# Seven block products instead of eight in a quarter of the gate and up projections of a transformer block on one Trainium2 core

## The chip, the cores and the metric

The kernel runs on one core of one Trainium2 chip. The time is device time in microseconds of one execution of the whole program. The engines are named as in the profile: PE (TensorE; PEld is its weight load), DVE (VectorE), ACT (ScalarE), POOL (GpSimd) and SP (SyncE, which here only issues DMAs).

## The reference

One encoder block on 256 rows of width 2048, in float32: a norm, four parallel mixers and an output projection, a cross-attention, and a gated feed-forward layer with 5632 hidden columns, then a last norm. The change lies in the feed-forward layer:

```python
def swiglu(h, w_gate_up, w_down):
    gate, up = jnp.split(h @ w_gate_up, 2, axis=-1)
    return (jax.nn.silu(gate) * up) @ w_down
```

Here `h` is 256x2048, `w_gate_up` 2048x11264 (5632 gate columns, then 5632 up columns) and `w_down` 5632x2048.

## The kernel before

**Products.** A float32 product is made of three matmuls on numbers rounded to a shorter type: each operand is a high part and a low part, and high*high + high*low + low*high are added in PSUM. For activations the two parts lie side by side in one tile of 512 columns: 256 columns high, 256 low (rows of `h` as columns). For weights ACT makes the high part `wh` (line 104) and DVE the low part `wl` (line 105).

**Weights.** All weight matrices come as one stream of 128x128 blocks in the order of use. A slab is 16 blocks (128x2048, 1 MB), loaded by SP into one of three `raw` buffers (line 83). Half a slab, 128x1024, is split at a time into one of three pairs of `wh` and `wl`. `take` (line 109) hands out 512 columns and sees to it that two more halves are written into the program ahead of the one in use.

**Gate and up.** `gate_up` (line 782) walks over 11 column blocks j of 512 hidden columns. For j = 0 gate and up run together in four PSUM banks (two row halves of 128 rows, and gate and up). For j = 1 to 10 first the gate block runs over all 16 inner blocks k, then the up block, each in two banks of the pool `psG`; `part_rows` (line 360) makes the three matmuls of 128x128 by 128x512 for one k and one row half. So one j has 16 k x 2 row halves x 2 (gate, up) x 3 = 192 matmuls. ACT turns the gate banks into silu (line 794); DVE multiplies them with the up banks (line 799, the operation in line 200), transposes the result in blocks (line 396), and POOL's queue stores it to the DRAM tensor `hidden` with four DMAs per row half (line 399).

**Down.** `down` multiplies with `w_down`, four column blocks c of 512, 44 inner blocks k each. The hidden activations are read back by `fetch` (line 803): a POOL DMA of 128x256 into `tmp`, then a split into a tile of `f` by ACT (line 204) and DVE (line 196). The first 28 of the 44 are read back during gate and up, the last 16 during down. At the top of `down` eight transposes of the residual go into two banks of the pool `psM` (line 889).

**Order.** Work that is not matrix product is written as generators, which `Background` (line 126) advances between products: `poll` runs a step when its due time has come and less than 0.9 us of DVE work is owed by the code's own count (`pe` takes time off, `dve` adds it); `drain` runs a generator to its end. That gives an order in the code. The tile framework then lays the instructions out on each engine with a planner of its own, and `keep_place` (line 222) pins instructions behind their predecessor where the planner is not to move them ahead.

Of the kernel before, what the change touches and what calls it, by code (L numbers as in the profile page):

```python
# [38 lines left out]
ROWS = ((0, 512), (704, 768), (880, 944), (NBLK - 48 * FT, NBLK))  # L39

LATE = 12

LAG, OWED, SOON = 1.3, 0.9, 0.01

NSC = 3
V_NG = 0
# [16 lines left out]
class Stream:  # L63
# [13 lines left out]
    def _half(self):  # L77

        nc, n = self.nc, 8 * len(self.halves)
        if n % 16 == 0:  # L80
            self.raw = self.rawp.tile([P, 2048], F32, name="raw", tag="raw")
            for a, b in zip(CUTS[n], CUTS[n][1:]) if n in CUTS else [(0, 1024), (1024, 2048)] if self.after else [(0, 2048)]:
                (nc.scalar if (n, a) == (0, 0) else nc.sync).dma_start(self.raw[:, a:b], self.W[n // 16][:, a:b])
                if self.after:
                    self.after.pop(0)()
        o = (n % 16) * P
# [12 lines left out]
        wh, wl = (pool.tile([P, 1088], F32R, name=t, tag=t) for t in ("wh", "wl"))  # L99
        at = 48 if any(a <= n < b for a, b in ROWS) else 8  # L100
        wh, wl = wh[:, at:at + 1024], wl[:, at:at + 1024]
        edges = [0, 256, 512, 1024] if n == 0 else [0, 512, 1024] if n == 8 else [0, 1024]
        for a, b in zip(edges, edges[1:]):
            nc.scalar.copy(wh[:, a:b], r[:, a:b])  # L104
            nc.vector.tensor_tensor(out=wl[:, a:b], in0=r[:, a:b], in1=wh[:, a:b].bitcast(F32), op=ALU.subtract)  # L105
        self.bg.dve(1024)
        self.halves.append((wh, wl))

    def take(self, w, k, c, nb=1):
        if self.n % 8 == 0:  # L110
            ahead = self.n // 8 + 1 + min(3 if self.extra else 2, self.n // 16)
            while len(self.halves) < min(ahead, NBLK // 8):
                self._half()
# [54 lines left out]
class Block:  # L168
# [191 lines left out]
    def part_rows(self, p, r, slot, wh, wl, start, stop, narrow=False):  # L360

        if narrow:
            for c in (slice(0, R), slice(R, 512)):
                self.part_rows(p[:, c], r, slot, wh[:, c], wl[:, c], start and c.start == 0, stop)
            return
        hi, lo = slot[:, r * P:(r + 1) * P], slot[:, R + r * P:R + (r + 1) * P]
        self.nc.tensor.matmul(p, hi, wh, start=start, stop=False)  # L367
        self.nc.tensor.matmul(p, hi, wl, start=False, stop=False)  # L368
        self.nc.tensor.matmul(p, lo, wh, start=False, stop=stop)  # L369
        self.bg.pe(0.68 * wh.shape[1] / 512)  # L370
# [399 lines left out]
    def mlp(self):  # L770
        tc, nc, act = self.tc, self.nc, self.act
        with tc.tile_pool(name="fp", bufs=1) as fp:
            self.gap(fp, 192)
            f = act[4:12] + [fp.tile([P, 512], F32R, name=f"f{i}") for i in range(20)] + self.h3
# [7 lines left out]
    def gate_up(self, gp, f):  # L782

        nc = self.nc
        box, g, stored = {}, {}, []

        def norm():
            box["col"] = self.rstd_begin([[self.acc]], D)
            yield

        def gate(ps):
            for r in range(2):
                g[r] = gp.tile([P, 512], F32, name=f"g{r}", tag=f"g{r}")
                nc.scalar.activation(g[r], ps[r], AF.Silu, scale=box["col"][:, r:r + 1])

        def up(j, ps):
            for r in range(2):
                h, u = (gp.tile([P, 512], F32, name=n, tag=n) for n in ("h", "u"))
                self.stt(h, ps[r], box["col"][:, r:r + 1], g[r], ALU.mult, ALU.mult)
                self.store_turned(self.ff[j * 512:(j + 1) * 512, r * P:(r + 1) * P], u, h)  # L800
            stored.append(j)

        def fetch(k0, k1, ahead, pause):

            m = {}
            for k in range(k0, k1 + ahead):
                if k < k1:
                    while len(stored) <= k // 4:
                        yield
                    m[k] = self.tmp()  # L810
                    nc.gpsimd.dma_start(m[k], self.ff[k * P:(k + 1) * P, :])  # L811
                if k >= k0 + ahead:
                    mark = self.mark()
                    self.split(f[k - ahead], m.pop(k - ahead))
                    self.keep_place(mark)
                    self.have = k - ahead + 1
                    yield pause

        ready = [self.late, self.bg.add(norm())]
        turned = self.bg.add(self.turn())  # L820
        ps = self.gemm_rows("w_gate_up", [0, DFF], self.h3, parts=[range(12), range(12, 16)],
                            before=lambda n: n and [self.bg.drain(g) for g in ready])
        gate(ps[0])
        up(0, ps[1])
        early = self.bg.add(fetch(0, FT - 16, 3, 2.0))
        for j in range(1, DFF // 512):
            gate(self.gemm_rows("w_gate_up", [j * 512], self.h3)[0])
            up(j, self.gemm_rows("w_gate_up", [DFF + j * 512], self.h3)[0])
        for x in (turned, early):
            self.bg.drain(x)  # L830
        self.bg.add(fetch(FT - 16, FT, 6, SOON))

    def turn(self):

# [19 lines left out]
    def down(self, f):  # L854
# [650 lines left out]
```

## Time and profile before

| what | value |
|---|---|
| runs | 1485.33, 1485.05, 1487.88 us (median 1485.33) |
| profiled execution, span from first to last instruction | 1482.6 us |
| profiled execution, its own time | not given apart from the span; the fastest run shown is 2.45 us above it |
| gate and up, j = 1 to 10, and a few transposes | 798.9 to 1234.8 us |
| down | 1234.8 to 1474 us |
| PE busy over the span | 99% |
| DVE / ACT busy over the span | 64% / 52% |

Matmul rows give about 389 ns for each matmul, but matmuls are pipelined: the distance from one start to the next is what adds up. A line number in a group is often a helper's, so tiles and shapes tell the groups apart. Two idle figures are to be kept apart: idle time of DVE or ACT costs nothing as long as PE has work.

### The profile page before, as it was taken

To read this page: it belongs to the slowest core of one execution; us is meant where nothing else is said; L and a number is where in the kernel's file an instruction comes from. 1 tells how busy PE (TensorE), PEld (TensorE's weight loads), DVE (VectorE), ACT (ScalarE), POOL (GpSimd) and SP (SyncE) were. 2 spreads that over 40 slices of the span, in tenths; PEclk is the share of its full clock that TensorE was granted. 3 is DMA by queue.
4 is the path that set the end of the run, shared out by engine and by line. 5 is a ranking of instruction groups with operands and counts; after the bars stand their busy time and mean duration, and the time that the engine had idled before them with its cause. 6 is when DMAs were issued, how large, how long until landed. Compare 5 with 4: busy or idle time off the path is not lost.

```text
span 1482.6 us, 19388 instructions
## 1 busy us (share of the span) xinstructions
PE 1468.6 (99%) x7356; PEld 1242.4 (84%) x7356; DVE 944.4 (64%) x1378; ACT 764.0 (52%) x1136; POOL 161.6 (11%) x276
## 2 busy tenths in 40 slices
PE   9999999999999999999999999999999999999997
PEld 8778888898898888888888888888888888888886
DVE  6688668778777777877765554555554456444444
ACT  6565655467555656656544444444444445434344
POOL 0220100000000001200042401111110112000000
PEclk9999999999999999999999999999999999999999
DMA  9976554454546555544567766666666666555554
GB/s 359 343 258 213 199 195 162 162 177 166 185 138 215 191 180 201 198 171 154 187 197 245 243 213 216 222 225 227 207 206 215 225 223 224 187 192 195 199 196 145
DMA packets 56718, 306.08 MB, mean 206 GB/s; under 512 B 9486, under 2 KB 11183, under 8 KB 25009
## 3 DMA queue, kind: packets, MB, share of 16 engines
q1 hardware_dynamic: 45920, 281.11, 55.1%
q0 software_dynamic: 10272, 23.09, 5.3%
q8 instruction: 57, 0.93, 0.3%
q10 hardware_dynamic: 432, 0.66, 0.1%
q14 instruction: 37, 0.30, 0.1%
HBM read 291.18 MB, written 13.63 MB: 206 GB/s over the span
## 4 chain that ended last, share of the span: by engine, by line
PE 97%; DVE 1%; ACT 1%; DMA 0%; SPq 0%; issue 0%; DVEq 0%; ACTq 0%
PE pg L368 20%; PE pg L367 20%; PE pg L369 20%; PE pg L318 18%; PE pg L319 10%; PE pm L369 1%; PE pm L368 1%; PE pm L367 1%; PE pm L1006 1%; PE pg L315 1%; PE pg L316 1%; PE pm L763 1%; PE pm L736 0%; DVE wl L105 0%; DMA raw<-in_W 0%; PE pm L1386 0%
## 5 line engine op out<-in xcount | busy, mean ns | idle before, releaser
L105 DVE TENSOR_TENSOR wl<-raw,wh 128x1024 fp32r<-128x1024 f32 (+1 forms) x503 | 611.4, 1217 | 465.1 <-ACT wh L104 459.9
L104 ACT CAST wh<-raw 128x1024 fp32r<-128x1024 f32 (+1 forms) x503 | 523.8, 1043 | 584.5 <-PE pg L369 415.4
L368 PE MATMUL pg<-wl,act 128*128 128x512 f32 (+1 forms) x1170 | 455.6, 389 | 1.5 <-DVE wl L105 1.5
L367 PE MATMUL pg<-wh,act 128*128 128x512 f32 (+1 forms) x1170 | 456.5, 390 | 0.0
L369 PE MATMUL pg<-wh,act 128*128 128x512 f32 (+1 forms) x1170 | 455.4, 389 | 0.0
L318 PE MATMUL pg<-act,wh 128*128 128x512 f32 x1104 | 387.7, 393 | 2.9 <-DVE act L196 2.9
L319 PE MATMUL pg<-act,wl 128*128 128x256 f32 x1216 | 340.7, 280 | 0.0
L368 PEld LDWEIGHTS pg<-wl,act 128*128 128x128 f32 x1170 | 219.9, 188 | 48.2 <-DVE wl L105 3.1
L367 PEld LDWEIGHTS pg<-wh,act 128*128 128x128 f32 x1170 | 219.9, 188 | 47.1 <-issue 1.2
L369 PEld LDWEIGHTS pg<-wh,act 128*128 128x128 f32 x1170 | 219.8, 188 | 45.8
L318 PEld LDWEIGHTS pg<-act,wh 128*128 128x128 f32 x1104 | 207.3, 188 | 48.1 <-DVE act L196 3.3
L319 PEld LDWEIGHTS pg<-act,wl 128*128 128x128 f32 x1216 | 228.5, 188 | 0.8 <-DVE wl L105 0.5
L399 POOL DMA_DIRECT2D hidden<-u x88 | 56.9, 654 | 304.1 <-DVE u L396 302.4
L369 PE MATMUL pg<-wh,f 128*128 128x512 f32 x120 | 46.7, 389 | 0.0
L367 PE MATMUL pg<-wh,f 128*128 128x512 f32 x120 | 46.7, 389 | 0.0
L368 PE MATMUL pg<-wl,f 128*128 128x512 f32 x120 | 46.7, 389 | 0.0
L843 POOL DMA_DIRECT2D xrows<-tmp x48 | 27.7, 584 | 128.8 <-DVE tmp L840 124.2
L196 DVE TENSOR_TENSOR tmp<-pg,tmp 128x256 f32<-128x256 f32 x78 | 32.4, 417 | 4.5 <-ACT tmp L325 3.7
L315 PE MATMUL pg<-act,wh 128*128 128x256 f32 x112 | 31.6, 282 | 0.0
L316 PE MATMUL pg<-act,wh 128*128 128x256 f32 x112 | 31.4, 280 | 0.0
L811 POOL DMA_DIRECT2D tmp<-hidden x44 | 24.3, 559 | 60.8 <-DMA hidden<-u 44.9
L399 POOL DMA_DIRECT2D keys<-k x32 | 20.7, 655 | 81.4 <-DVE k L396 79.2
(293 smaller groups left out, 1201.1 us busy)
## 6 DMA issues: line engine op xcount, KB each, us to landing
raw<-in_W SPq DMA_DIRECT2D x246, 1024.0 KB, 5.0
raw<-in_W SPq DMA_DIRECT2D x11, 512.0 KB, 7.3
hidden<-u POOLq DMA_DIRECT2D x88, 64.0 KB, 3.2
tmp<-hidden POOLq DMA_DIRECT2D x44, 128.0 KB, 3.1
res<-in_xT SPq DMA_DIRECT2D x8, 512.0 KB, 7.6
k<-in_mem SPq DMA_DIRECT2D x8, 256.0 KB, 8.3
k<-in_x SPq DMA_DIRECT2D x8, 256.0 KB, 10.2
keys<-k POOLq DMA_DIRECT2D x32, 64.0 KB, 5.2
```

Of the source, the lines that this page charges most:

```text
L104: nc.scalar.copy(wh[:, a:b], r[:, a:b])
L105: nc.vector.tensor_tensor(out=wl[:, a:b], in0=r[:, a:b], in1=wh[:, a:b].bitcast(F32), op=ALU.subtract)
L196: self.nc.vector.tensor_tensor(out=out, in0=a, in1=b, op=op)
L315: self.nc.tensor.matmul(p[:, 0:R], wh, slot[:, 0:R], start=start, stop=False)
L316: self.nc.tensor.matmul(p[:, 0:R], wh, slot[:, R:512], start=False, stop=False)
L318: self.nc.tensor.matmul(p[:, :], wh, slot[:, :], start=start, stop=False)
L319: self.nc.tensor.matmul(p[:, 0:R], wl, slot[:, 0:R], start=False, stop=stop)
L367: self.nc.tensor.matmul(p, hi, wh, start=start, stop=False)
L368: self.nc.tensor.matmul(p, hi, wl, start=False, stop=False)
L369: self.nc.tensor.matmul(p, lo, wh, start=False, stop=stop)
L399: nc.gpsimd.dma_start(to[:, :, 32 * a:32 * a + 32], u[32 * a:32 * a + 32, :].rearrange("f (b t) -> f b t", t=32))
L843: nc.gpsimd.dma_start(to[:, :, c:c + 32], u[32 * a:32 * a + 32, :].rearrange("t (b f) -> t b f", f=32))
```

## The change

The inner dimension of gate and up is 16 blocks, that is 8 pairs of blocks. For j = 1 to 10 gate and up now run together, pair by pair, in four PSUM banks. Pairs 1 and 5 of the eight are no longer done as eight block products (2 row halves x 2 inner blocks x gate and up) but as the seven products of Strassen's scheme (in Winograd's form), each again three matmuls.

- The slabs of these pairs are not split in halves. `_forms` makes from the slab three of its own blocks and four sums of its blocks, each as high and low part, into single-buffered tiles `hb`, `lb`, `ht`, `lt`, with the sums in float32 in `t`.
- The sums of the activations that the scheme needs are made once, during j = 0, by `left`.
- Three of the seven products go straight into the banks of the result, four into four banks of their own, which `combine` adds up behind pair 5. So one j uses all eight banks; the two pools change roles from one j to the next.
- The end of each j (`finish`) adds the combined products to the result banks, then silu, product, transposes and stores; its steps are spread by `poll` over the start of the next j, and drained ahead of pair 1 of it.
- 16 of the 44 blocks of the hidden activations, not 28, are read back during gate and up, 28 during down; the tiles for 12 of them lie in the space that gate and up leave free.

```diff
+EARLY = 16
+GU = 16 * (40 + 16 + 16 + 32 + 16)
+SEVEN = (1, 5)
+def seven(slab):
+    j, i = divmod(slab - GU // 16, 8)
+    return 1 <= j < DFF // 512 and i in SEVEN
...
+    def _forms(self, raw):
+        nc = self.nc
+        hb, lb, ht, lt = (self.swp.tile([P, w], F32R, name=t, tag=t)
+                          for t, w in (("hb", 1536), ("lb", 1536), ("ht", 2048), ("lt", 2048)))
+        t = self.swp.tile([P, 2048], F32, name="t", tag="t")
+        blk = raw.rearrange("p (b c) -> p b c", b=4)
+        sub = lambda out, a, b: nc.vector.tensor_tensor(out=out, in0=a, in1=b, op=ALU.subtract)
+        nc.scalar.copy(hb, raw[:, 512:2048])
+        sub(t[:, 0:1024].rearrange("p (b c) -> p b c", b=2), blk[:, 1:4:2, :], blk[:, 0:1, :].to_broadcast([P, 2, 512]))
+        nc.scalar.copy(ht[:, 0:1024], t[:, 0:1024])
+        nc.vector.tensor_tensor(out=t[:, 1024:1536], in0=raw[:, 1536:2048], in1=t[:, 0:512], op=ALU.add)
+        sub(t[:, 1536:2048], raw[:, 1024:1536], t[:, 1024:1536])
+        nc.scalar.copy(ht[:, 1024:2048], t[:, 1024:2048])
+        sub(lb, raw[:, 512:2048], hb.bitcast(F32))
+        for a in (0, 1024):
+            sub(lt[:, a:a + 1024], t[:, a:a + 1024], ht[:, a:a + 1024].bitcast(F32))
+        self.bg.dve(5632, 6)
...
-            with tc.tile_pool(name="gp", bufs=2) as gp:
-                self.gate_up(gp, f)
+            with tc.tile_pool(name="sw", bufs=1) as sw, tc.tile_pool(name="gp", bufs=1) as gp:
+                self.st.swp = sw
+                self.gate_up(sw, gp, f)
...
+                f += [hp.tile([P, 512], F32R, name=f"g{i}") for i in range(FT - 16 - EARLY)] + self.h3
+                self.bg.add(self.fetch(f, EARLY, FT, 6, SOON))
...
+        def left():
+            for i in SEVEN:
+                t = [self.tmp() for _ in range(2)]
+                for x, k in zip(t, (2 * i, 2 * i + 1)):
+                    nc.scalar.activation(x, self.resk(k), AF.Copy, scale=self.gvec(V_NG + 32, k))
...
+        def unit(i, cs, ps, start, stop, c0, c1):
+            b11, b21, b22, u1, t3, t2, t4 = st.take_forms("w_gate_up", (2 * i, 2 * i + 1), c0, c1)
+            whole = lambda k, r: [self.h3[k][:, a + r * P:a + (r + 1) * P] for a in (0, R)]
+            formed = lambda n: [x[:, n * P:(n + 1) * P] for x in sums[i]]
+            for p, a, b, own in ((ps[0], whole(2 * i, 0), b11, True), (cs[0][0], whole(2 * i + 1, 0), b21, False),
+                                 (cs[0][1], formed(3), b22, False), (ps[1], formed(0), u1, True), (ps[2], formed(2), t3, True),
+                                 (ps[3], formed(1), t2, True), (cs[1][0], whole(2 * i + 1, 1), t4, False)):
+                self.part(p, *a, *b, own and start, own and stop)
+                self.bg.poll()
+        def combine(ps, s):
+            p1, p5, p7, p6 = ps
+            (g0, u0), (g1, u1) = s
+            m = gp.tile([P, 512], F32, name="m", tag="m")
+            nc.scalar.copy(g0, p1)
+            self.tt(m, p6, g0, ALU.add)
+            yield SOON
+            self.tt(u0, p5, m, ALU.add)
+            yield SOON
+            self.tt(g1, p7, m, ALU.add)
+            yield SOON
+            self.tt(u1, p5, g1, ALU.add)
+        def finish(j, cs, s, last):
...
+                if last:
+                    self.tt(s[r][0], cs[r][0], s[r][0], ALU.add)
+                nc.scalar.activation(s[r][0], s[r][0] if last else cs[r][0], AF.Silu, scale=box["col"][:, r:r + 1])
...
+        for j in range(DFF // 512):
+            cols = [j * 512, DFF + j * 512]
+            banks = [self.gbank, self.bank]
+            cs = [[banks[j % 2]() for _ in cols] for _ in range(2)]
...
+                if i == 1 and end:
+                    self.bg.drain(end)
+                if j and i in SEVEN:
+                    if i == SEVEN[0]:
+                        ps = [banks[1 - j % 2]() for _ in range(4)]
+                    unit(i, cs, ps, i == SEVEN[0], i == SEVEN[-1], *cols)
```

More of the change, by code (lines that the diff above doesn't have):

```diff
@@ L85, in _half @@
                     self.after.pop(0)()
+        if seven(n // 16):
+            self.halves += [self._forms(self.raw), None]
+            return
         o = (n % 16) * P
@@ L107, in _half, with take_forms, look @@
         self.halves.append((wh, wl))
+    def _forms(self, raw):
[15 more added lines that the diff above has]
+        self.bg.dve(5632, 6)
+        cut = lambda x, y: [(x[:, a:a + 512], y[:, a:a + 512]) for a in range(0, x.shape[1], 512)]
+        return cut(hb, lb) + cut(ht, lt)
+    def take_forms(self, w, ks, c0, c1):
+        assert self.n % 16 == 0 and seven(self.n // 16)
+        self.look()
+        forms = self.halves[self.n // 8]
+        for k, c in ((ks[0], c1), (ks[0], c0), (ks[1], c0), (ks[1], c1)):
+            self.order += [(w, k, c + i * P) for i in range(4)]
+        self.n += 16
+        self.halves[self.n // 8 - 2] = None
+        return forms
+    def look(self):
+        ahead = self.n // 8 + 1 + min(3 if self.extra else 2, self.n // 16)
+        while len(self.halves) < min(ahead, NBLK // 8):
+            self._half()
     def take(self, w, k, c, nb=1):
         if self.n % 8 == 0:
-            ahead = self.n // 8 + 1 + min(3 if self.extra else 2, self.n // 16)
-            while len(self.halves) < min(ahead, NBLK // 8):
-                self._half()
+            self.look()
         half, o = self.halves[self.n // 8], (self.n % 8) * P
@@ L365, in part_rows, with part @@
             return
-        hi, lo = slot[:, r * P:(r + 1) * P], slot[:, R + r * P:R + (r + 1) * P]
+        self.part(p, slot[:, r * P:(r + 1) * P], slot[:, R + r * P:R + (r + 1) * P], wh, wl, start, stop)
+    def part(self, p, hi, lo, wh, wl, start, stop):
         self.nc.tensor.matmul(p, hi, wh, start=start, stop=False)
@@ new lines, in combine @@
+        def combine(ps, s):
[12 more added lines that the diff above has]
+            if last:
+                yield from last
@@ L803, in fetch @@
[L803 to L817, printed above, removed]
+                g, h = s[r]
@@ new lines, in finish @@
+                if last:
+                    self.tt(h, cs[r][1], h, ALU.add)
+                    yield SOON
+            for r in range(2):
+                g, h = s[r]
+                u = gp.tile([P, 512], F32, name="u", tag="u", bufs=2)
+                self.stt(h, h if last else cs[r][1], box["col"][:, r:r + 1], g, ALU.mult, ALU.mult)
+                yield SOON
+                self.store_turned(self.ff[j * 512:(j + 1) * 512, r * P:(r + 1) * P], u, h)
+                yield SOON
+            self.stored.append(j)
@@ L819, in gate_up @@
         ready = [self.late, self.bg.add(norm())]
+        forms = self.bg.add(left())
         turned = self.bg.add(self.turn())
[L821 to L828, printed above, removed]
@@ L829, in gate_up @@
-        for x in (turned, early):
+        early = end = None
+        for j in range(DFF // 512):
+            cols = [j * 512, DFF + j * 512]
+            banks = [self.gbank, self.bank]
+            cs = [[banks[j % 2]() for _ in cols] for _ in range(2)]
+            last = None
+            if j == 1:
+                self.bg.drain(forms)
+                early = self.bg.add(self.fetch(f, 0, EARLY, 3, 2.0))
+            for i in range(8):
+                if j == 0 and i == 6:
+                    for g in ready:
+                        self.bg.drain(g)
+                if i == 1 and end:
[4 more added lines that the diff above has]
+                    unit(i, cs, ps, i == SEVEN[0], i == SEVEN[-1], *cols)
+                    if i == SEVEN[-1]:
+                        s = [[gp.tile([P, 512], F32, name=f"{n}{r}", tag=f"{n}{r}") for n in "gh"] for r in range(2)]
+                        last = combine(ps, s)
+                        self.bg.add(last)
+                    continue
+                for k in (2 * i, 2 * i + 1):
+                    for c in range(2):
+                        wh, wl = st.take("w_gate_up", k, cols[c], 4)
+                        for r in range(2):
+                            self.part_rows(cs[r][c], r, self.h3[k], wh, wl, k == 0, k == KT - 1)
+                            self.bg.poll()
+            if j == 0:
+                s = [[gp.tile([P, 512], F32, name=f"{n}{r}", tag=f"{n}{r}") for n in "gh"] for r in range(2)]
+            else:
+                self.bg.drain(last)
+            end = self.bg.add(finish(j, cs, s, last))
@@ L830, in gate_up @@
+        for x in (end, turned, early):
             self.bg.drain(x)
-        self.bg.add(fetch(FT - 16, FT, 6, SOON))
     def turn(self):
```

43 lines of the change are left out of this document (32 added, 11 removed).

## The prediction

> **What bounds the kernel now.** I read the page first, then the chain of work that ended last around the stage, then busy time by stretch, groups by shape, VectorE's timeline and the waits.
>
> ```profile
> span 1482.6 us, 19388 instructions
> PE 1468.6 (99%) x7356; PEld 1242.4 (84%) x7356; DVE 944.4 (64%) x1378; ACT 764.0 (52%) x1136; POOL 161.6 (11%) x276
> PEclk9999999999999999999999999999999999999999
> PE 97%; DVE 1%; ACT 1%; DMA 0%; SPq 0%; issue 0%; DVEq 0%; ACTq 0%
> ```
>
> ```profile
> 798.91 0.44 PE pm L889 x4
> 799.35 0.47 PE pg L367
> ...
> 1234.58 0.23 PE pg L369
> 1234.82 0.44 PE pm L889 x4
> 1235.26 0.24 PE pg L367
> ```
>
> The chain is PE for 97% of the span, at full clock throughout. j = 1 to 10 run on PE from 799.35 to 1234.82 with no wait: 435.47 us for 10 x 192 matmuls, 0.2268 us from start to start. One j takes 43.55 us, a pair of inner blocks 24 matmuls or 5.44 us, a half slab 2.72 us. A removed matmul is worth 0.2268 us as long as everybody else keeps up.
>
> The second thing in these rows matters as much. Line 889's eight transposes stand at the top of `down`; four of them ran at 798.91, 436 us ahead of their place in the code. So the planner lays work out by when it is ready, not by the order of the code.
>
> How busy the others are, in one j (columns: PE, PEld, DVE, ACT, POOL busy, clock, DMA share, GB/s), with and without reading back hidden activations, and in `down`:
>
> ```profile
> 1016.60:1060.20 43.60, 43.60 (x194) 36.12 (x193) 23.45 (x25) 19.25 (x22) 7.38 (x12) 1.00 0.64 217
> ...
> 1147.40:1191.00 43.60, 43.60 (x194) 36.12 (x193) 22.10 (x21) 18.02 (x18) 7.37 (x12) 1.00 0.64 217
> ```
>
> ```profile
> 1300.00:1360.00 60.00, 60.00 (x266) 49.70 (x265) 28.49 (x27) 24.27 (x26) 0.00 (x0) 1.00 0.57 193
> ```
>
> VectorE works 23.45 of 43.60 us (54%) and, as the timeline further down shows, idles 1.49 us ahead of each split. That spare half is what the change spends.
>
> **PE.** Per pair the change removes one product of eight, 3 matmuls; 2 pairs x 10 j x 3 = 60 matmuls x 0.2268 = **-13.6 us**. The new pair takes 21 x 0.2268 = 4.76 us, one j 42.19. Weight loads are one per matmul as before and 188 ns long (a row below), under the 227 of a matmul, so they do not take over.
>
> **VectorE per j.** Prices:
>
> ```profile
> L105 DVE TENSOR_TENSOR wl<-raw,wh 128x1024 fp32r<-128x1024 f32 x145 | 177.3, 1223 | 185.9 <-ACT wh L104 185.9
> L104 ACT CAST wh<-raw 128x1024 fp32r<-128x1024 f32 x144 | 150.8, 1047 | 213.2 <-PE pg L369 213.2
> L369 PEld LDWEIGHTS pg<-wh,act 128*128 128x128 f32 x577 | 108.3, 188 | 22.5
> L399 POOL DMA_DIRECT2D hidden<-u x72 | 46.5, 654 | 256.4 <-DVE u L396 254.7 <-issue 1.7
> L200 DVE SCALAR_TENSOR_TENSOR h<-pg,rc,g 128x512 f32<-128x512 f32 x18 | 12.6, 742 | 0.0
> L794 ACT ACTIVATE g<-pg,rc 128x512 f32<-128x512 f32 x18 | 12.3, 690 | 8.0 <-PE pg L369 8.0
> L396 DVE STREAM_TRANSPOSE u<-h 128x512 f32<-128x512 f32 x18 | 11.6, 683 | 0.0
> L196 DVE TENSOR_TENSOR f<-tmp,f 128x256 fp32r<-128x256 f32 x20 | 8.2, 417 | 0.0
> L204 ACT CAST f<-tmp 128x256 fp32r<-128x256 f32 x20 | 7.9, 402 | 0.0
> ```
>
> ```profile
> L196 DVE TENSOR_TENSOR res<-res,pg 128x512 f32<-128x512 f32 x2 | 1.3, 678 | 0.0
> ```
>
> From 417 ns at 256 columns and 1223 at 1024 a column costs 1.05 ns, so 1536 columns are an estimated 1.76 us; 512 columns are 0.68 (last row, one input in PSUM, as in `combine` and `finish`).
> - Removed: 4 half slabs, 4 x 1.22 = 4.9. Left: 12 x 1.22 = 14.7.
> - Added: forms of two slabs, each 3 x 1.22 + 2 x 0.68 + 1.76 = 6.8, together 13.6; four adds in `combine`, 2.7; four in `finish`, 2.7.
> - Unchanged: two products 1.48, two transposes 1.37, and up to four splits of read-back blocks, 1.67.
> - Sum 36.5, with splits 38.2, of 42.19 us: 87 to 91%; operations that follow at once overlap by about 0.08 (two products take 1.40, below, for 1.48), which makes it 81 to 85%. It fits, with 4 to 8 us left per j where 20 were.
>
> The step with a price that no row shows is the 1024-column subtraction that reads one block twice (a broadcast input). Bounds: 1.22, and 2.45 if it ran at half rate; I take 1.22, since its form differs from line 105 only in the addresses read. At 2.45 VectorE has 2.5 us more per j, which still fits.
>
> **ScalarE per j.** 12 x 1.05 + 2 x (1.47 + 2 x 1.05) + 2 x 0.69 for silu + 0.62 for one copy + 4 x 0.40 = 23.3 us of 42.19. The 1.47 (1536 columns) and 0.62 (512) go by 402 ns at 256 and 1047 at 1024. Beside PE: 0. If its cover were gone, 23.3 - 19.25 = 4 us per j.
>
> **When it must be done.** Time 0 is the last matmul of the j before.
>
> ```profile
> 1016.75 1.40 DVE L200 SCALAR_TENSOR_TENSOR h<-pg,rc,g 128x512 f32<-128x512 f32 x2
> 1018.07 1.29 DVE L396 STREAM_TRANSPOSE u<-h 128x512 f32<-128x512 f32 x2
> ...
> 1031.93 1.23 DVE L105 TENSOR_TENSOR wl<-raw,wh 128x1024 fp32r<-128x1024 f32 x1 [1.49 <-ACT wh L104]
> ```
>
> ```profile
> SPq L83 <- DVE wl L105: 821.4, 161, 12.3
> ```
>
> ```profile
> DMA to landing us min/median/max: 4.8/4.9/5.6
> ```
>
> SP waits only for a free slab buffer. The slab of pair 1 takes that of the slab three earlier (pair 6), whose second half is split two halves ahead of its use at -8.2, so by about -13.6 + 1.05 + 1.22 = -11.3; 4.9 us later, at -6.4, the new slab lies there. Pair 1 starts at 5.44. Within these 11.8 us VectorE owes: two half-slab splits 2.4, the three forms' sums and `lb` 4.4 (the first products need these), and the first add of `finish` 0.68, which frees the bank that pair 1 starts in. That is 7.5 of 11.8. By the end of pair 1 (10.2) it also owes the other two split steps of the forms 2.4, three adds 2.0, products and transposes 2.85 and the next half slab or two 2.4: 17.2 of 16.6 us, some 15.9 after overlaps. So the first deadline is loose and the second has 0.7 us to spare: this is the place where the change can fail. Pair 5 has only forms ahead of it, no `finish`.
>
> Here I choose. Lost per j at pair 1: at least 0, at most 4.6 (worked out in the first rival). The nearest row is the pair `h`, `h`, then `u`, `u` above: the code writes product, transpose, product, transpose, and the planner put the second product into the time in which the first transpose was not ready. With that and the four early transposes I take a planner that fills gaps, and 0.2 us per j for orders that fit badly: **+2.0 us**.
>
> **What moves.** Twelve of the read-backs go from gate and up to `down`: 12 POOL issues, 12 casts (0.40) and 12 splits (0.42) in a stage where VectorE has 28.5 of 60 us and POOL nothing to do: 0; uncovered, 12 x 0.42 = 5 us. Their tiles lie where gate and up's tiles were, the last of which are given back when the last stores have left: 8 x 0.654 = 5.2 us of POOL issues after the last transpose, so about 11 us into `down`, while block 16 is needed after 16 x 6 x 0.2268 = 21.8 us. On POOL's queue they stand behind those stores, as the last read-backs do now. `left` adds about 3.6 us of VectorE and 2.8 of ScalarE to j = 0: covered, 0. At the top of `down`, the second result bank is freed by `finish`'s third add, about 0.1 + 3 x 0.68 = 2.1 us after the last matmul; transposes (0.88 if all eight come here) and three matmuls (0.68) cover 1.6: **+0.5** (bounds 0, and 5.5 for the whole of `finish`). SP issues the same slabs; with no wait in its way, 0.
>
> **Sum.** -13.6 + 2.0 + 0.5 = -11.1: a span of 1471.5. The median of the runs is 2.7 us above the profiled span, so 1474.
>
> **Rivals.**
> (1) Slower: VectorE keeps the code's order at pair 1. There the whole of the forms stands ahead of `finish`, since the code owes 6.8 us from them and so polls none of `finish` until it is drained. Forms then begin after the split at -0.4 and some 2.7 us of leftover adds, at 2.3, end at 8.7 (6.4 with overlaps), and the first add at 9.4: pair 1 starts 4.0 late, and the half slab behind `finish` comes 0.6 late again. 4.6 x 10 - 13.6 = +32: 1518. Against it: the two reorderings above. It decides once more than 1.36 us per j is lost, and above 3 us waits the order must really be the code's. [...]
> (2) The order is filled, but VectorE, at 85%, slips by 0.5 to 1.8 us per j at the second deadline (a broadcast at half rate, or waits between dependent forms, would do it): about 1.0 x 10, so 1482.
> (3) The change brings less than its count: matmuls slow down as VectorE and ScalarE fill up. For: nothing; j with 23.45 and with 22.10 us of VectorE take the same 43.60. 5 ns per matmul over 1860 is 9 us: 1483.
>
> **Chances.** Forecast (1471 to 1478) 0.50; (2) 0.24; (1) and states between (1490 to 1518) 0.19; (3) 0.07. A difference under 0.2%, 3 us, can hardly be told from none: the three runs shown differ by that much. Faster: 0.50, 0.13 of (2) and 0.03 of (3); same: 0.07 and 0.03; the rest slower. The likeliest case's own range is 1471 to 1478. Downwards nothing is left beyond the 60 matmuls, 1471; upwards the range takes in (2), (3) and the lower part of (1), to 1500, and leaves out the rest of (1) and a little below.
>
> **What would show it.** Matmuls of the stage fewer by 60 and 42.2 to 42.4 us per j; VectorE 33 to 38 us busy in each; the wait of PE on `lb`, on `finish`'s adds and on `wl` behind pair 1 near zero. The chain leaving PE for VectorE ahead of pair 1, or `finish` standing behind the forms in VectorE's timeline, shows (1) or (2); a longer step between matmuls without waits shows (3). The read-backs should not appear in the chain in `down`.

## The result, and the profile after

| | median us | runs | lowest to highest |
|---|---|---|---|
| before | 1486.49 | 13 | 1485.05 to 1489.13 |
| changed | 1481.33 | 13 | 1477.87 to 1484.97 |

The ratio is 0.9966, with a 95% interval of 0.9956 to 0.9976: the change makes the kernel faster by 5.2 us. The forecast was 11.3 us (1485.33 to 1474). So the sign held, and so did the wide range, up to 1500; the forecast's own range, 1471 to 1478, did not, and more than half of the gain is missing. The sections below look for that half.

The page of the changed kernel: its span, the busy time of each engine, the granted clock in 40 slices, and the shares of the chain of work that ended last, by engine and by line.

```profile
span 1479.6 us, 19468 instructions
...
PE 1459.8 (99%) x7296; PEld 1230.8 (83%) x7296; DVE 1066.3 (72%) x1548; ACT 793.3 (54%) x1172; POOL 161.4 (11%) x276
...
PEclk9999999999999999999999999999999999999999
...
PE 75%; DVE 12%; DMA 8%; issue 3%; ACT 2%; SPq 0%; DVEq 0%; ACTq 0%
PE pg L370 18%; PE pg L422 11%; PE pg L423 11%; PE pg L421 11%; PE pg L371 10%; DMA raw<-in_W 8%; DVE wl L121 5%; PE pm L423 2%; PE pm L422 2%; PE pm L421 2%; DVE t L133 2%; DVE lt L133 2%; DVE lb L133 1%; PE pm L1145 1%; ACT wh L120 1%
```

The matmuls are fewer by 60 (7356 to 7296), as counted. But the chain, which was PE for 97% of the span, now leaves PE for VectorE (12%: the split of half slabs, `wl`, and the forms' `t`, `lt`, `lb`) and for the slab transfers (8%). (The lines have moved: the split of a half slab is now L120 on ACT and L121 on DVE, the three matmuls of a product are L421, L422 and L423, the forms' sums are L133.)

Where the stage ends, in the chain of the changed kernel (start us, us, what):

```profile
1231.06 0.24 PE pg L423
1231.30 0.87 PE pm L1028 x8
1232.17 0.23 PE pg L421
```

All eight transposes (line 889 before, 1028 now) stand at the top of `down`, and the next product follows at once. j = 1 to 10 start at 801.36 and end at 1231.30: 429.94 us for 1860 matmuls, which at 0.2268 us would take 421.85. **8.1 us are lost in these ten j.** The distances between successive starts of matmuls show the same: what they have beyond 0.2268 us, called PE's gaps from here on, adds up to 7.5 us, all of it at line 422, the first product of a half slab with its low part `wl`, and at the matmul right behind it.

So the balance of the two profiled spans, 1482.6 and 1479.6, is this. Gate and up with j = 0 and the eight transposes went from 480.4 us (754.9 to 1235.26) to 474.7 (757.5 to 1232.17): 5.7 us won. `down` took 247.3 before and 247.4 after. And the stage began 2.6 us later, which is lost before the first changed instruction; the last section comes back to that.

The list of waits over the changed kernel's run (engine, line, what was waited for: us in total, times, longest):

```profile
DVE t L133 <- DMA raw<-in_W: 58.7, 20, 5.2
ACT hb L134 <- DMA raw<-in_W: 55.3, 18, 7.3
...
PE pg L422 <- DVE wl L121: 4.3, 7, 1.5
...
PE pm L422 <- DVE wl L121: 2.7, 4, 1.1
```

The first two rows have no counterpart before. In every one of the 20 uses of the scheme VectorE stands at the forms' first subtraction and waits for the slab's transfer, 2.9 us on average; ScalarE does the same in 18 of them at the forms' first cast. The last two rows are PE's waits for `wl`.

Busy time in about one j and in a later one (columns as in the prediction):

```profile
931.00:975.00 44.00, 42.64 (x186) 34.42 (x185) 34.86 (x42) 21.84 (x27) 7.37 (x12) 1.00 0.63 215
1018.00:1060.00 42.00, 42.00 (x187) 34.79 (x186) 34.11 (x38) 21.77 (x23) 7.39 (x12) 1.00 0.66 234
```

VectorE is busy for 34 us of a j, within the 33 to 38 of the prediction; the second stretch has no gap on PE at all. The load is the one that was worked out. What is wrong is the order. One place shows it: the end of the first of these stretches. The changed kernel's timelines of ScalarE, VectorE and PE (start us, us, engine, line, operation; in brackets the idle time before it, and what ended it):

```profile
961.96 1.05 ACT L120 CAST wh<-raw 128x1024 fp32r<-128x1024 f32 x1 [3.21 <-DMA raw<-in_W]
...
963.22 0.58 ACT L899 COPY g<-pm 128x512 f32<-128x512 f32 x1
968.77 1.48 ACT L134 CAST hb<-raw 128x1536 fp32r<-128x1536 f32 x1 [4.98 <-DMA raw<-in_W]
970.15 1.05 ACT L136 CAST ht<-t 128x1024 fp32r<-128x1024 f32 x1
971.11 1.04 ACT L120 CAST wh<-raw 128x1024 fp32r<-128x1024 f32 x1
```

```profile
964.52 0.68 DVE L248 TENSOR_TENSOR m<-pm,g 128x512 f32<-128x512 f32 x1
968.79 1.23 DVE L133 TENSOR_TENSOR t<-raw 128x1024 f32<-128x1024 f32 x1 [3.59 <-DMA raw<-in_W]
...
972.93 1.22 DVE L121 TENSOR_TENSOR wl<-raw,wh 128x1024 fp32r<-128x1024 f32 x1
```

```profile
972.84 0.39 PE L421 MATMUL pg<-wh,act 128*128 128x512 f32 x1
974.20 0.50 PE L422 MATMUL pg<-wl,act 128*128 128x512 f32 x1 [0.97 <-DVE wl L121]
```

The slab of pair 7 landed just ahead of 961.96, when ScalarE cast its first half. Its second half lay there from then on, and by 964 ScalarE had nothing else to do. But the next instruction in its queue is `hb` of the following pair 1, whose slab lands only at 968.7. ScalarE stands 4.98 us, VectorE 3.59 us and, in the middle of `combine`, the other three adds with it. When the slab lands, `hb`, `ht`, three steps of `t` and three adds go first, the split of pair 7's second half ends at 974.15, and PE has waited since the product of 972.84.

The other gaps are alike. All ten places where PE waits for `wl` in these ten j lie at the third or the second half slab ahead of a pair with forms (the last half of pair 7 or the first of pair 0, the last of pair 3 or the first of pair 4). For six of them the trace gives the landing of the slab: it was there 9 to 13 us before PE came to it.

### The profile page after: what moved, and what is told of

Read it like the earlier page. It is cut to its first block, busy times and chain, and to the rows that moved or that the text cites. A ratio compares the mean times of both kernels' runs of the same rounds, so it can differ in the third digit from the quotient of the medians.

```text
span 1479.6 us, 19468 instructions
## 1 busy us (share of the span) xinstructions
PE 1459.8 (99%) x7296; PEld 1230.8 (83%) x7296; DVE 1066.3 (72%) x1548; ACT 793.3 (54%) x1172; POOL 161.4 (11%) x276
## 4 chain that ended last, share of the span: by engine, by line
PE 75%; DVE 12%; DMA 8%; issue 3%; ACT 2%; SPq 0%; DVEq 0%; ACTq 0%
PE pg L370 18%; PE pg L422 11%; PE pg L423 11%; PE pg L421 11%; PE pg L371 10%; DMA raw<-in_W 8%; DVE wl L121 5%; PE pm L423 2%; PE pm L422 2%; PE pm L421 2%; DVE t L133 2%; DVE lt L133 2%; DVE lb L133 1%; PE pm L1145 1%; ACT wh L120 1%
## 5 line engine op out<-in xcount | busy, mean ns | idle before, releaser
L121 DVE TENSOR_TENSOR wl<-raw,wh 128x1024 fp32r<-128x1024 f32 (+1 forms) x463 | 559.4, 1214 | 269.2 <-ACT wh L120 264.1
L120 ACT CAST wh<-raw 128x1024 fp32r<-128x1024 f32 (+1 forms) x463 | 480.6, 1042 | 473.7 <-PE pg L423 219.8
L422 PE MATMUL pg<-wl,act 128*128 128x512 f32 (+1 forms) x770 | 300.3, 390 | 4.4 <-DVE wl L121 4.3
L421 PE MATMUL pg<-wh,act 128*128 128x512 f32 (+1 forms) x770 | 300.8, 391 | 0.1
L423 PE MATMUL pg<-wh,act 128*128 128x512 f32 (+1 forms) x770 | 299.7, 389 | 0.0
L422 PEld LDWEIGHTS pg<-wl,act 128*128 128x128 f32 x770 | 144.6, 188 | 38.0 <-DVE wl L121 8.3
L421 PEld LDWEIGHTS pg<-wh,act 128*128 128x128 f32 x770 | 144.5, 188 | 31.9 <-issue 1.2
L423 PEld LDWEIGHTS pg<-wh,act 128*128 128x128 f32 x770 | 144.5, 188 | 29.9
L422 PE MATMUL pm<-wl,act 128*128 128x512 f32 x272 | 106.6, 392 | 2.8 <-DVE wl L121 2.7
L423 PE MATMUL pm<-wh,act 128*128 128x512 f32 x272 | 105.9, 389 | 0.0
L421 PE MATMUL pm<-wh,act 128*128 128x512 f32 x272 | 105.9, 389 | 0.0
L133 DVE TENSOR_TENSOR t<-raw 128x1024 f32<-128x1024 f32 x20 | 24.5, 1225 | 58.7 <-DMA raw<-in_W 58.7
L422 PEld LDWEIGHTS pm<-wl,act 128*128 128x128 f32 x272 | 51.1, 188 | 15.8 <-DVE wl L121 5.2
L134 ACT CAST hb<-raw 128x1536 fp32r<-128x1536 f32 x20 | 29.6, 1480 | 60.4 <-DMA raw<-in_W 55.3
L421 PEld LDWEIGHTS pm<-wh,act 128*128 128x128 f32 x272 | 51.1, 188 | 10.7
L423 PEld LDWEIGHTS pm<-wh,act 128*128 128x128 f32 x272 | 51.1, 188 | 10.3
L133 DVE TENSOR_TENSOR lt<-t,ht 128x1024 fp32r<-128x1024 f32 x40 | 48.0, 1216 | 0.0
```

The source lines that it names most:

```text
L133: sub = lambda out, a, b: nc.vector.tensor_tensor(out=out, in0=a, in1=b, op=ALU.subtract)
L134: nc.scalar.copy(hb, raw[:, 512:2048])
```

## The experiments

The theories, by the letters of the expectations. **W**: the planner put the forms' first cast and first subtraction too early in the two queues; both stand there until the slab has landed, and half slabs whose data is there stand behind them. **L**: VectorE has too much work in one j, above all in the first five, in which hidden activations are read back. **S**: the new structure itself (gate and up together, four or eight banks, the later read-backs) costs something. Ratios are to the kernel before, on the same chip, with their 95% interval.

### The forms pinned behind the half slab ahead of them

```diff
+        mark = len(nc.cur_bb.bb.instructions)
         nc.scalar.copy(hb, raw[:, 512:2048])
         sub(t[:, 0:1024].rearrange("p (b c) -> p b c", b=2), blk[:, 1:4:2, :], ...)
+        for x in nc.cur_bb.bb.instructions[mark:]:
+            if x.engine in self.behind:
+                self.tc.add_manual_dep(x, self.behind[x.engine], mybir.DependencyInfo(
+                    mybir.DependencyClass.NoSync, mybir.DependencyReason.DATA), reason="order")
...
         self.bg.dve(1024)
+        if n % 16 == 0:
+            self.behind = {x.engine: x.name for x in nc.cur_bb.bb.instructions[-2:]}
```

The two instructions may not be laid out ahead of the split of the first half slab of the pair before; no wait is added, only an order within a queue.

> The first cast and the first subtraction of a slab's forms are pinned behind the split of the first half slab of the pair before, so that they no longer stand early in their queues. Theory W (the queues of ScalarE and VectorE stand behind an operation that waits for its slab's transfer, 58.7 us in all, and the half-slab splits behind it come late): VectorE's waits for the slab fall under 10 us, PE's gaps in gate and up from 7.6 us to under 2, the time some 5 us below the changed kernel, a ratio of 0.992 to 0.9935 to the kernel before. Theory L (VectorE has too much work in one j, above all while hidden activations are read back): the waits go, the gaps stay, since the work is the same; 0.9966. Theory S (the new order by pairs, with four banks and all of the evacuation at the end of j, costs by itself): the gaps stay; 0.9966.

Measured: 1473.96 us, ratio **0.9912** (0.9898 to 0.9926), a span of 1471.9. Waits for the slab over the run:

```profile
ACT hb L137 <- DMA raw<-in_W: 5.4, 9, 2.1
...
DVE t L135 <- DMA raw<-in_W: 0.8, 1, 0.8
```

And VectorE's timeline at the same place of another j:

```profile
1008.51 1.23 DVE L121 TENSOR_TENSOR wl<-raw,wh 128x1024 fp32r<-128x1024 f32 x1 [1.49 <-ACT wh L120]
1009.66 1.22 DVE L135 TENSOR_TENSOR t<-raw 128x1024 f32<-128x1024 f32 x1
1010.80 1.75 DVE L135 TENSOR_TENSOR lb<-raw,hb 128x1536 fp32r<-128x1536 f32 x1
```

VectorE's waits for the slab fall from 58.7 to 0.8 us, ScalarE's from 55.3 to 5.4, PE's gaps in j = 1 to 10 from 7.5 to 0.3, and the time falls by 7.4 us against the changed kernel (1481.33 to 1473.96), a little more than W expected. VectorE is as busy as in the changed kernel. W stands: the same work in another order loses nothing.

### The new structure without the scheme

```diff
-SEVEN = (1, 5)
+SEVEN = ()
...
-            else:
+            elif last:
                 self.bg.drain(last)
+            else:
+                s = [[gp.tile([P, 512], F32, name=f"{n}{r}", tag=f"{n}{r}") for n in "gh"] for r in range(2)]
```

> No pair by seven products; all else of the change stays (order by pairs, four banks, the end of j in one piece, 16 blocks read back early). W and L: nothing waits and VectorE has no forms, so 0.999 to 1.001 of the kernel before, no gaps on PE. S: slower than the kernel before, up to 1.005, with gaps of some 7 us.

Measured: 1486.04 us, ratio 0.9996 (0.9987 to 1.0005), no gaps in the stage. S falls: gate and up together, the changing banks and twelve read-backs moved to `down` cost nothing that can be measured.

### The read-backs spread out

```diff
-                early = self.bg.add(self.fetch(f, 0, EARLY, 3, 2.0))
+                early = self.bg.add(self.fetch(f, 0, EARLY, 3, 12.0))
```

> The 16 early read-backs come with a pause of 12 us instead of 2, so their splits spread over most of the ten j. L: the gaps in the first four j go, at most 2 us are left in all; 0.9925 to 0.9935. W: the waits for the slab stay at 50 to 60 us, the gaps shrink a little where the queue behind the wait is shorter, to 4 to 6 us; 0.995 to 0.9965. S: 0.9966.

Measured: 1483.53 us, ratio 0.9979 (0.9971 to 0.9988). The waits over the run:

```profile
DVE t L133 <- DMA raw<-in_W: 70.3, 20, 5.5
...
ACT hb L134 <- DMA raw<-in_W: 65.1, 19, 7.2
```

PE's gaps grew from 7.5 to 12.0 us in the profiled execution (at 1486.59 us the longest of its eleven). L expected them at 2 us or less, W at 4 to 6: both were missed. Where the added gaps lie is shown two experiments further down.

### The scheme in pair 5 alone

```diff
-SEVEN = (1, 5)
+SEVEN = (5,)
```

> Only pair 5 of each j by seven products: 30 matmuls fewer, 6.8 us of PE, and 5.5 us less of VectorE's work per j than with two pairs. L: VectorE has 31 us of work in 42.9, no gaps: all 6.8 us arrive, 0.9954, as good as or better than two pairs. W: half of the waits (25 to 30 us) and about half of the gaps (3 to 4 us): 0.9975 to 0.998. S: the gaps stay at 7 us: 1.000.

Measured: 1480.09 us, ratio 0.9958 (0.9944 to 0.9971), gaps of about 0.9 us. The waits over the run:

```profile
ACT hb L134 <- DMA raw<-in_W: 15.6, 10, 2.8
DVE t L133 <- DMA raw<-in_W: 3.5, 4, 1.6
```

W's number here, which left part of the loss in place, was missed, and L's, 0.9954, was the one met: 30 matmuls are worth 6.8 us, and 6.1 (1486.15 to 1480.09) arrive. By itself this run can't tell less work from shorter waits; the first experiment, with the work of both pairs and no gaps, does. With one pair the planner happens to put the forms where they hardly wait, 3.5 us in ten uses against 58.7 in twenty. So the changed kernel, with two pairs, is as fast as one with the scheme in one pair: what the second pair saves on PE, 6.8 us, goes into its gaps.

### The early read-backs moved behind gate and up

```diff
-                early = self.bg.add(self.fetch(f, 0, EARLY, 3, 2.0))
+                pass
...
-        for x in (end, turned, early):
+        self.bg.drain(end)
+        early = self.bg.add(self.fetch(f, 0, EARLY, 3, SOON))
+        for x in (turned, early):
             self.bg.drain(x)
```

All read-backs are still done; none runs beside gate and up.

> Nothing is read back while j = 1 to 10 run: the 16 early blocks are read back all at once between gate and up and down, which makes that place longer by some 10 us and is not what is looked at. Looked at are PE's gaps from j = 1 to 10. If a wait for the slab is enough by itself (W alone): the waits stay at 50 to 60 us and the gaps at 5 to 7. If gaps need both the wait and a queue that is full (W with L): the waits stay at 45 to 60 us and the gaps fall to 2 or less.

Measured once: 1485.18 us, beside 1486.18 of the kernel before; part of it is lost at the crowded top of `down`, with two gaps of 1.39 us and matmuls 0.43 us apart behind them. What it was run for is the stage itself:

```profile
DVE t L133 <- DMA raw<-in_W: 58.0, 17, 5.4
...
ACT hb L134 <- DMA raw<-in_W: 53.1, 16, 6.9
```

The waits over the run are what they were, and PE's gaps in j = 1 to 10 are 6.3 us. L falls, also as a condition of W: the read-backs aren't needed for the loss.

But they add to it where the queues stand. In this run and in the one with the read-backs spread out, VectorE's operations in gate and up come in the same order, by the tiles that they read and write, and so do ScalarE's, once those of the read-back blocks are left out. Beyond 42.19 us for each j, j = 1 to 4 lose 6.4 us here and 6.2 there; j = 5 to 10 lose 0.2 us here, where nothing is read back, and 6.9 there, where nine blocks are. Whether it is the blocks' splits or their transfers isn't separated.

### VectorE and ScalarE in the order of the code

```diff
+        prev = {}
+        for x in nc.cur_bb.bb.instructions[first:]:
+            if x.engine in (mybir.EngineType.DVE, mybir.EngineType.Activation):
+                if x.engine in prev:
+                    self.tc.add_manual_dep(x, prev[x.engine], mybir.DependencyInfo(
+                        mybir.DependencyClass.NoSync, mybir.DependencyReason.DATA), reason="order")
+                prev[x.engine] = x.name
```

This pins every instruction of the two engines in gate and up behind the one that the code writes before it: the prediction's first rival, built.

> VectorE's and ScalarE's instructions of j = 1 to 10 are pinned in the order of the code. The prediction's first rival: pair 1 starts 4.0 us late and the half slab behind it 0.6 more in each j, 4.6 x 10 - 13.6 = +32 us, a ratio of 1.02. If waits of PE for the first adds of the end of j are shorter than that, 1.00 to 1.01. If the order does not matter, 0.9966.

Measured: 1496.54 us, ratio 1.0069 (1.0054 to 1.0084), the only version slower than before. VectorE's and PE's timelines at a new j's pair 1:

```profile
1075.54 2.35 DVE L133 TENSOR_TENSOR lt<-t,ht 128x1024 fp32r<-128x1024 f32 x2
1077.81 1.28 DVE L248 TENSOR_TENSOR g<-pg,g 128x512 f32<-128x512 f32 x2
...
1083.00 3.46 DVE L121 TENSOR_TENSOR wl<-raw,wh 128x1024 fp32r<-128x1024 f32 x3
```

```profile
1081.85 1.07 PE L421 MATMUL pm<-wh,act 128*128 128x512 f32 x4
...
1084.23 0.50 PE L422 MATMUL pm<-wl,act 128*128 128x512 f32 x1 [1.31 <-DVE wl L121]
```

Here `finish` (line 248) stands behind the forms, as the rival said, and the splits of the next half slabs behind `finish`. One j takes 43.90 us (862.27 to 1213.47 for eight), 1.71 above the 42.19 of its matmuls. But the rival had priced 4.6: 4.0 ahead of pair 1 and 0.6 behind it. Pair 1 starts in time, since PE began with its products that need no freed bank, and the loss lies at the half slab behind pair 1, as in the second row (1.31 us idle), some 1.4 us each. Another 6.0 us are one single gap at 818.7. It is the same loss with another transfer: in the code's order the cast of the first read-back stands ahead of the next `wh`, and ScalarE waits 14.1 us for its data.

```profile
823.54 0.40 ACT L256 CAST act<-tmp 128x256 fp32r<-128x256 f32 x1 [14.12 <-DMA tmp<-hidden]
```

### Only one engine pinned

```diff
-            if x.engine in self.behind:
+            if x.engine in self.behind and x.engine == mybir.EngineType.DVE:
```

This is the first experiment with VectorE's instruction alone pinned; the second of the pair has `Activation` in the place of `DVE`.

> As e1, but only VectorE's first subtraction of the forms is pinned, not ScalarE's cast. If VectorE's wait is what costs: gaps under 2 us, 0.991 to 0.993. If ScalarE's (the casts of half slabs stand behind it): VectorE's wait under 10 us, ScalarE's at 50 us and more, gaps 5 to 7 us, 0.996 to 0.997. If both: between.

> As e1, but only ScalarE's cast is pinned. If VectorE's wait is what costs: it stays at 50 to 60 us, gaps 5 to 7 us, 0.996 to 0.997. If ScalarE's: gaps under 2 us, 0.991 to 0.993. If both: between.

Measured: 1481.69 us with VectorE pinned, ratio 0.9969 (0.9958 to 0.998), gaps 7.3 us; 1482.39 with ScalarE pinned, ratio 0.9974 (0.9959 to 0.9989), gaps 10.7. Both are where the changed kernel is: each came out as the branch of its expectation in which the other engine's wait is what costs. The waits of the two, over the run:

```profile
ACT hb L137 <- DMA raw<-in_W: 60.3, 20, 5.9
...
DVE lb L135 <- ACT hb L137: 42.9, 20, 4.2
```

```profile
ACT ht L143 <- DVE t L135: 83.7, 18, 7.9
...
DVE t L135 <- DMA raw<-in_W: 62.9, 20, 7.8
```

Either engine alone held up the half slabs here. With VectorE free of the wait for the slab, ScalarE still stands at `hb`; `wl` needs `wh` from ScalarE, so the loss stays. With ScalarE pinned, VectorE stands at `t`, and ScalarE behind it at `ht`.

### A buffer of their own for the slabs of pairs 1 and 5

```diff
-            self.raw = self.rawp.tile([P, 2048], F32, name="raw", tag="raw")
+            pool, tag = (self.swp, "own") if seven(n // 16) else (self.rawp, "raw")
+            self.raw = pool.tile([P, 2048], F32, name=tag, tag=tag)
```

Nothing is pinned; the transfer of such a slab waits for the forms before it, about half a j earlier, and no longer for the split of a slab shortly before. To make room, 12 blocks instead of 16 are read back early.

> The slabs of pairs 1 and 5 are loaded into a buffer of their own instead of one of the three shared ones (and 12 blocks, not 16, are read back early, to make room). Nothing is pinned. If the waits come from a shared buffer that comes free too late: the slab lands earlier, VectorE's waits for it fall under 15 us, gaps under 2 us, 0.991 to 0.993. If they come from the planner placing the first subtraction where it believes the slab to be there, whenever that is: the waits stay at 30 us or more; the gaps may still shrink, because there is more time behind them.

Measured: 1473.79 us, ratio 0.9922 (0.9907 to 0.9937). The wait for the slab, over the run:

```profile
DVE t L134 <- DMA own<-in_W: 16.7, 10, 2.2
```

The wait is a little above the 15 us that were expected. No gap is left in j = 1 to 10 (one of 1.6 us stands in `down`). The loss is gone here with no pin, as W says it should be when the slab is earlier in memory. But the planner laid the queues out otherwise too (VectorE's order in gate and up is another one in most places), so the earlier slab isn't shown to be the cause by itself.

### Three pairs, pinned

The pin of the first experiment, with `SEVEN = (1, 3, 6)` and 14 early blocks.

> Pinned as e1, with three pairs (1, 3 and 6) by seven products (14 blocks read back early, to make room). PE: 30 matmuls fewer than e1, -6.8 us. VectorE per j: 36.5 + 6.8 - 2 x 1.22 = 40.9 us of work, some 38 after overlaps, of 40.8 us. If filling VectorE to that point costs by itself (L): gaps of 1 us and more per j, no faster than e1, 0.991 to 0.998. If only waits cost (W): 0.9865 to 0.988.

Measured: 1466.12 us (1464.18 to 1468.12), ratio **0.9869** (0.9852 to 0.9885), the fastest version. Busy time over eight j:

```profile
870.00:1206.00 336.00, 336.00 (x1484) 278.25 (x1483) 310.71 (x336) 186.36 (x190) 50.81 (x81) 1.00 0.64 223
```

VectorE is busy 310.7 of 336 us, 92%, and PE is never without work. The waits over the run are not gone:

```profile
ACT hb L137 <- DMA raw<-in_W: 31.9, 11, 3.8
...
DVE t L135 <- DMA raw<-in_W: 8.1, 10, 1.9
```

So here neither VectorE's load, 92%, nor a wait as such, 31.9 us in all on ScalarE, cost PE time. In the changed kernel a wait cost where a half slab that was due soon stood behind it, 7.5 us in the ten j.

## Why the prediction was right and wrong

**Right: PE's count.** 60 matmuls went, at 0.2268 us from start to start, and the rate stayed. With the gaps gone the first experiment wins 12.2 of the 13.6 us (1486.15 to 1473.96), and three pairs win 19.3 of 20.4. The third rival, matmuls that slow down beside fuller engines, is out: at 92% of VectorE the 336 us above hold 1484 matmuls, 0.2264 us each.

**Right: VectorE's prices and load.** The broadcast subtraction, for which 1.22 us was chosen between 1.22 and 2.45, takes 1.225 in the changed kernel's groups by shape (count, then total us and mean ns, then idle time before it and what ended it):

```profile
L133 DVE TENSOR_TENSOR t<-raw 128x1024 f32<-128x1024 f32 x20 | 24.5, 1225 | 58.7 <-DMA raw<-in_W 58.7
...
L134 ACT CAST hb<-raw 128x1536 fp32r<-128x1536 f32 x20 | 29.6, 1480 | 60.4 <-DMA raw<-in_W 55.3
```

The right-hand column, idle time on line 133, is the part that the price list left out.

**Right: what was costed at nothing.** The moved read-backs cost nothing (second experiment, 0.9996). That experiment leaves `left` out; in the changed kernel j = 0, where `left` runs, takes 44.2 us (757.15 to 801.36), as before (754.51 to 798.75). SP's slabs, put at nothing too, come back below. The top of `down` cost 0.1 rather than the 0.5 forecast.

**Wrong: "0.2 us per j for orders that fit badly: +2.0 us".** This term of the sum measured 7.5 us by the gaps and 8.1 by the length of the ten j. It was placed at pair 1's deadlines, the form sums and `finish` against a slab that lies there at -6.4 on the clock of the j before. In the place shown above the slab landed even earlier, at 968.7 against a last matmul at 976.6, so at -7.9; and pair 1 itself was not late. What failed is the assumption behind the term: that VectorE and ScalarE come to the forms when the slab is there, and until then do what is ready. They came to them 3.6 and 5.0 us before. The early transposes and the pair `h`, `h`, `u`, `u` were read as a planner that fills gaps and so as a reason for a small price. But at the row `[4.98 <-DMA raw<-in_W]` ScalarE filled nothing: it stood 4.98 us ahead of `hb`, while the slab of the `wh` cast behind it had landed before 961.96. VectorE stood 3.59 us with three adds behind its subtraction. In the code's order ScalarE stood 14.12 us at the cast of the first read-back. So what was laid out behind a late transfer came late in these places, in the planner's order as in the code's. That the planner goes by when it expects data to be ready, and lays the forms out for a slab that then comes later, is the author's estimate: what time it supposes for a transfer no view shows.

**A second part of it, the transfer.** The prediction took 4.9 us from issue to landing, the median before. In the changed kernel, between 842 and 1215 us:

```profile
DMA to landing us min/median/max: 4.8/6.3/8.9
```

and with the forms pinned, over the same stretch:

```profile
DMA to landing us min/median/max: 4.9/5.6/7.3
```

The SP queue of the changed kernel, at the place shown above, has the two slabs ahead of pair 1's:

```profile
955.53 0.33 SPq L96 DMA_DIRECT2D raw<-in_W  x1
...
956.62 0.33 SPq L96 DMA_DIRECT2D raw<-in_W  x1
```

Before, SP issued 8 slabs in 38.41 us, one each 5.5 us by the rate at which PE used them up. Now a buffer comes free after the forms' last subtraction and the next after a split, and the two transfers, issued 1.09 us apart, run beside each other; the one that pair 7 waited for was there, by the start of its cast, 6.4 us after its issue. So slabs land later, which lengthens the wait. How much of the 7.5 us this is was not taken apart.

**The rivals.** (1), the code's order, is right in kind: built, it is slower than before. Its price, 4.6 us per j, was 2.7 times the 1.71 measured (the single gap of 6.0 us, which it didn't foresee, stands apart), because it let pair 1 wait for banks that its first products don't need; the place that binds is the half slab behind pair 1, which the prediction named as the second deadline. (2) forecast 1482 us and the time is 1481.3, but not for its reasons: the broadcast is not at half rate, and VectorE at 92% keeps up where the order is right. The agreement is by chance.

**The base.** The sum was set on three runs, 1485.33; the median of 13 is 1486.49. In each run of the comparisons the time stands 1.8 us above its own span; the profiled execution before, with 1482.6, was thus a quick one of about 1484.4. The forecast's 2.7 us between span and median held 0.9 us for that, and the median of 13 asks for 1.2 more. So 1474 + 5.7 (8.1 rather than 2.0 in j = 1 to 10, 0.1 rather than 0.5 at the top of `down`) + 1.2 = 1480.9, beside 1481.3 measured.

**Open.** Why j = 1 to 4 lose time even with nothing read back, while later j with the same waits lose none; whether a read-back adds its gap by its splits or by its transfer; how much of the loss is the longer transfers; and what duration the planner assumes for a slab.

## What to carry to other kernels

When a planner lays out the queues, price a new operation that reads a transfer by what will stand behind it if the transfer is late, not by its duration and the engine's load: here a VectorE at 92% cost nothing, and two early instructions in each use cost 7.5 us, the gain of a whole pair (6.8). Look in the waits for operations that idle on a DMA in every use, and follow the queue behind them to work whose data has long been there. Then either pin the first instruction behind work that is due sooner, on every engine that has one (one of the two alone gained nothing here), or start the transfer earlier.

## What the runs showed of the hardware

**Behind some waits of PE, of 1.39 to 6.0 us, matmuls went on at about half their rate, and not in every execution.** Between 475 and 480 us, long before the change, PE waits 2.94 us in the kernel before and 2.95 in the changed one. What follows, by stretch, before and then after:

```profile
478.00:490.00 12.00, 11.53 (x66) 10.16 (x67) 9.27 (x20) 6.74 (x14) 0.00 (x0) 1.00 0.59 195
```

```profile
479.00:490.00 11.00, 10.46 (x51) 9.14 (x52) 6.73 (x15) 4.74 (x10) 0.00 (x0) 0.84 0.41 144
```

In the execution before the clock stays at 1.00; in the one after it is 0.84 over 11 us, and for some of them matmuls start every 0.43 us rather than every 0.23. That is 1.6 of the 2.6 us by which the stage began later (the other 1.07 went on the first slabs of the kernel). The profiles of five experiments show this drop too: 0.91 over 475 to 495 us with the forms pinned, without the scheme and with one pair, 0.83 with the read-backs spread out, and 0.84 over 479 to 490 with three pairs. The structure without the scheme, which has the drop, takes the time of the kernel before, which has none in its profile (0.9996). With ScalarE pinned and with the buffer of its own j = 1 starts at 798.90 and 799.20 us, in the other eight at 800.23 to 801.55; by that these two are estimated to be without the drop, and it belongs to the execution rather than to the change. With ScalarE pinned the clock falls at another place, after a gap of 2.71 us at 817.3:

```profile
817.00:821.00 4.00, 1.46 (x6) 0.86 (x6) 3.91 (x5) 2.69 (x3) 2.22 (x4) 1.00 0.29 79
821.00:825.00 4.00, 4.00 (x12) 3.12 (x11) 4.00 (x4) 2.58 (x3) 0.00 (x0) 0.57 0.85 314
```

A clock of 0.57 over 4 us is an estimated 3.4 us at half clock, and matmuls stand 0.43 us apart from 821.85 to 824.83. Behind the one 6.0 us gap of the code's order they stand 0.43 us apart from 826.80 to 831.06, and 0.23 from there on. The same follows two gaps of 1.39 us close together; in the run without read-backs beside gate and up they end at 1232.15 and 1234.57:

```profile
1234.00:1237.50 3.50, 2.93 (x7) 2.35 (x8) 3.50 (x12) 1.17 (x4) 3.45 (x6) 0.51 0.38 82
```

The clock of 0.51 goes with matmuls 0.43 us apart from 1235.59 to 1237.30. What decides whether the clock falls behind a wait is not shown: 2.94 us left it at 1.00 in one profile, and 2.95 us were followed by the drop in another. The gaps at `wl` in the changed kernel, 1.3 us at most, left the clock at 1.00 in each stretch of j = 1 to 10, so the loss at the half slabs is the gaps themselves.
